# A decoder trunk in split float32: squares placed behind joins, pairs evacuated one behind the other, and norm sums taken by transposes

## The chip, the core and the metric

The kernel runs on one core of a Trainium2 chip. The metric is the device time of one execution in microseconds. Five engines work side by side, each through its own queue of instructions: PE (matrix products; its weight loads are listed as PEld), DVE (vector work), ACT (activations and copies), POOL and SP, which issues most DMAs. An instruction can wait for a semaphore that another engine raises; what stands behind it on its own engine waits with it.

## What is computed

Two layers of a decoder over 256 tokens of width 1024. Each layer is a half SwiGLU step, a token mixer, a cross attention over a memory of 256 rows, and a second half SwiGLU step, each behind an RMSNorm. The change concerns the norm and the first half step:

```python
def rmsnorm(x, g):
    x32 = x.astype(jnp.float32)
    y = x32 * lax.rsqrt(jnp.mean(x32 * x32, axis=-1, keepdims=True) + EPS)
    return y.astype(x.dtype) * g

def swiglu(x, w_gate, w_up, w_down):
    return (jax.nn.silu(x @ w_gate) * (x @ w_up)) @ w_down
...
    for l in range(DEPTH):
        x = x + 0.5 * swiglu(rmsnorm(x, ffn1_norm[l]), ffn1_w_gate[l], ffn1_w_up[l], ffn1_w_down[l])
```

The hidden width of SwiGLU is 2816, that is 22 column blocks of 128.

## The kernel before, in words

**Layout and products.** x lies transposed, as 8 row tiles of 128 features by 256 tokens. Every float32 factor is split into a high and a low part of a faster type: `hi` is a rounding copy on ACT, `lo` the difference on DVE. A product of a 128x128 weight tile with an x tile is then two matmuls (`mm`, L382 and L383): the high weight with both parts of x side by side, 512 columns, and the low weight with the high part of x, 256 columns. One column block takes 8 weight tiles, so 8 such pairs. `join` (L391) adds the two halves of the accumulator: ACT copies one half to SBUF (L392), DVE adds the other (L393).

**The weights.** `Stream` brings them in 1 MB chunks through SP into `raw` (4 buffers) and splits blocks of 8 tiles: `piece` issues the rounding copy `whi` on ACT (L127) and the difference `wlo` on DVE (L128). There are 5 buffers of each. `ws.fill()` splits the next block that is due, `ws.flush()` all that are due, `ws.take()` hands out a tile. Where in the code `fill` is called decides which other instructions the split is recorded among.

**The first half step** (`ffn` with `first=True`). `gates` computes the gate columns of blocks f0 to f3 in four accumulators while x and the weights still arrive. Then `gate_up` runs up f0, up f1, up f2, up f3, gate f4, up f4, gate f5, up f5, gate f6, up f6 and so on; each gets one of four `acc` buffers in PSUM and, once joined, one of eight `w1` buffers in SBUF. The products use x before it is normed; the norm's factor per token, `n.rbc`, is multiplied in afterwards. So a pair (gate, up) cannot be finished, nor its `w1` buffers freed, before `n.rbc` is there: `when_scaled` keeps its `evac` waiting. `evac(f)` is: gate times rbc (DVE, L516), silu (ACT, L517), `ws.fill()`, times up (DVE, L519), `ws.fill()`, and the split of the result into `h` (ACT L450, DVE L451).

**The norm's factor.** `squares` squares tiles of x on ACT (L327 two tiles at a time, L337 one) and adds them on DVE into one 128x256 tile, `sqacc`. `norm_scale` then makes the sum over the 128 partitions: `sums` multiplies each half of `sqacc` with a column of ones on PE (L346), DVE turns the two columns into mean plus epsilon (L348), POOL takes the power of minus one half (`rcol`, L350); `spread` transposes the broadcast `rcol` on PE (L356) and ACT copies it out as `rbc` (L358). The same function serves nine norms in the program, one of them that of the memory rows.

**What sets the order.** The program is recorded in the order of a hand-made planner (`Order`, method `after(delay, fn, cost)`, in planner nanoseconds): in the first half step, the squares are planned at 12000 to 17400, the sums at 18900. A scheduler then orders each engine's queue from a timing model of its own, keeping data dependencies; `tc.keep_in_program_order` takes an instruction out of that freedom. The cross attention (`attend_all`) has a step `go_weigh` that weights the values (L716 to L718).

## Time and profile before

| | us |
|---|---|
| median of 3 runs | 970.91 (970.76 to 971.05) |
| the profiled execution | 970.36 |
| its span, first to last instruction | 968.6 |
| PE busy in the span | 960.3 (99%) |
| DVE busy | 758.4 (78%) |
| ACT busy | 614.5 (63%) |
| POOL busy | 56.1 (6%) |

A row of the timeline gives start, duration, engine, line, operation, output and inputs, how many equal instructions were merged (x2), and in brackets how long the engine stood idle before it and what ended that. Durations overlap a little, since engines are pipelined: the distance between two starts is what a queue really takes. A row of the groups gives the count, then busy time and the mean in ns of one. PEclk is the granted clock of PE, 1.00 being full.

### The profile page before, as it was taken

The page shows a single profiled execution, that of the slowest core. Times are in us where ns is not written, and L with a number is a line of the kernel's source. Part 1 is how long each engine was busy: PE and PEld are TensorE (multiplying, and loading weights), DVE is VectorE, ACT ScalarE, POOL GpSimd, SP SyncE. Part 2 cuts the span into 40 slices and gives each one's busy share as a digit, 9 for nine tenths or more (in the row PEclk, how much of TensorE's full clock was granted, in tenths as well). Part 3 has the DMA queues.
Part 4 walks back from the last instruction along what each step waited for, and adds up shares of the span by engine and source line. Part 5 has one row for each costly group of instructions (what it writes and reads, how often), then busy time and mean ns, then how long its engine had stood idle before and what let it go on. Part 6 is the DMA issues. An engine that isn't in the chain of part 4 may idle for free.

```text
span 968.6 us, 16929 instructions
## 1 busy us (share of the span) xinstructions
PE 960.3 (99%) x6552; PEld 901.4 (93%) x6552; DVE 758.4 (78%) x1353; ACT 614.5 (63%) x1144; POOL 56.1 (6%) x95
## 2 busy tenths in 40 slices
PE   9999999999999999999999999999999999999997
PEld 8899999999999999999999999999999999999896
DVE  7988767798878888876778878677878789888663
ACT  7767655697658766665556666556786677666541
POOL 0410000002000000000000000000000004400011
PEclk9999999999999999999999999999999999999999
DMA  9797556555545665556555565565645357765631
GB/s 373 276 328 286 188 204 212 171 186 181 201 139 200 215 202 211 201 194 215 185 206 195 198 216 184 209 202 190 220 140 192 123 175 246 250 238 185 213 131 44
DMA packets 29921, 196.73 MB, mean 203 GB/s; under 512 B 3848, under 2 KB 4872, under 8 KB 7184
## 3 DMA queue, kind: packets, MB, share of 16 engines
q1 hardware_dynamic: 27072, 187.44, 55.6%
q0 software_dynamic: 2192, 7.37, 2.2%
q8 instruction: 51, 0.84, 0.4%
q10 hardware_dynamic: 576, 0.83, 0.2%
q14 instruction: 30, 0.25, 0.1%
HBM read 193.51 MB, written 5.27 MB: 205 GB/s over the span
## 4 chain that ended last, share of the span: by engine, by line
PE 99%; DVE 1%; ACT 0%; issue 0%; POOLq 0%; DVEq 0%; ACTq 0%
PE acc L382 42%; PE acc L383 21%; PE acc L387 7%; PE acc L389 7%; PE acc L388 7%; PE acc L565 1%; PE acc L564 1%; PE acc L563 1%; PE acc L905 1%; PE acc L907 1%; PE acc L906 1%; PE sc L563 0%; PE sc L565 0%; PE sc L564 0%; PE tr L289 0%; PE tr L740 0%
## 5 line engine op out<-in xcount | busy, mean ns | idle before, releaser
L127 ACT ACTIVATE whi<-raw 128x1024 fp32r<-128x1024 f32 (+2 forms) x377 | 369.5, 986 | 271.4 <-PE acc L382 132.0
L128 DVE TENSOR_TENSOR wlo<-raw,whi 128x1024 fp32r<-128x1024 f32 (+2 forms) x377 | 426.7, 1136 | 145.7 <-ACT whi L127 143.0
L382 PE MATMUL acc<-x,whi 128*128 128x512 f32 x1392 | 457.5, 383 | 0.5 <-DVE w L393 0.5
L383 PE MATMUL acc<-x,wlo 128*128 128x256 f32 x1392 | 377.6, 273 | 0.6 <-DVE wlo L128 0.6
L382 PEld LDWEIGHTS acc<-x,whi 128*128 128x128 f32 x1392 | 262.3, 189 | 36.8 <-PE acc L383 0.8
L383 PEld LDWEIGHTS acc<-x,wlo 128*128 128x128 f32 x1392 | 267.4, 192 | 1.8 <-DVE wlo L128 0.9
L382 PE MATMUL acc<-h,whi 128*128 128x512 f32 x462 | 151.3, 382 | 0.0
L383 PE MATMUL acc<-h,wlo 128*128 128x256 f32 x462 | 125.5, 273 | 0.0
L382 PEld LDWEIGHTS acc<-h,whi 128*128 128x128 f32 x462 | 87.1, 189 | 12.0
L383 PEld LDWEIGHTS acc<-h,wlo 128*128 128x128 f32 x462 | 88.7, 192 | 0.2
L388 PE MATMUL acc<-h,whi 128*128 128x256 f32 x322 | 87.8, 275 | 0.0
L389 PE MATMUL acc<-h,wlo 128*128 128x256 f32 x322 | 87.8, 275 | 0.0
L387 PE MATMUL acc<-h,whi 128*128 128x256 f32 x322 | 86.5, 277 | 0.0
L393 DVE TENSOR_TENSOR w<-acc,w 128x256 f32<-128x256 f32 x195 | 81.2, 417 | 3.8 <-ACT w L392 3.5
L389 PE MATMUL acc<-x,wlo 128*128 128x256 f32 x304 | 84.1, 278 | 0.0
L388 PE MATMUL acc<-x,whi 128*128 128x256 f32 x304 | 84.0, 278 | 0.0
L387 PE MATMUL acc<-x,whi 128*128 128x256 f32 x304 | 83.2, 278 | 0.0
L392 ACT ACTIVATE w<-acc 128x256 f32<-128x256 f32 x195 | 71.8, 369 | 9.2 <-PE acc L383 9.1
L388 PEld LDWEIGHTS acc<-h,whi 128*128 128x128 f32 x322 | 61.7, 192 | 0.1
L389 PEld LDWEIGHTS acc<-h,wlo 128*128 128x128 f32 x322 | 61.7, 192 | 0.1
L387 PEld LDWEIGHTS acc<-h,whi 128*128 128x128 f32 x322 | 60.6, 192 | 0.4 <-DVE x L445 0.2
L388 PEld LDWEIGHTS acc<-x,whi 128*128 128x128 f32 x304 | 58.2, 192 | 0.2
(207 smaller groups left out, 1181.5 us busy)
## 6 DMA issues: line engine op xcount, KB each, us to landing
raw<-in_w SPq DMA_DIRECT2D x171, 1024.0 KB, 5.0
dists<-line POOLq DMA_DIRECT2D x2, 1536.0 KB, 14.7
raw<-in_memT SPq DMA_DIRECT2D x3, 1024.0 KB, 4.9
raw<-in_w SPq DMA_DIRECT2D x6, 384.0 KB, 6.5
bias<-dists POOLq DMA_DIRECT2D x2, 1024.0 KB, 13.1
x<-in_xT SPq DMA_DIRECT2D x1, 1024.0 KB, 7.6
tok<-q POOLq DMA_DIRECT2D x32, 32.0 KB, 3.6
bias<-tok POOLq DMA_DIRECT2D x1, 1024.0 KB, 6.2
```

The lines of the kernel that those rows point to most:

```text
L127: for ins in (self.nc.scalar.activation(hi[:, at], src, AF.Copy), self.nc.vector.tensor_tensor(lo[:, at], src, hi[:, at].bitcast(F32), op= ...
L128: self.nc.vector.tensor_tensor(lo[:, at], src, hi[:, at].bitcast(F32), op=ALU.subtract)):
L382: nc.tensor.matmul(ps, w[0], x2.both, start=start, stop=False)
L383: nc.tensor.matmul(ps[:, :S], w[1], x2.high, start=False, stop=stop)
L387: nc.tensor.matmul(ps[:, :S], w[0], x2.high, start=start, stop=False)
L388: nc.tensor.matmul(ps[:, :S], w[0], x2.low, start=False, stop=False)
L389: nc.tensor.matmul(ps[:, :S], w[1], x2.high, start=False, stop=stop)
L392: nc.scalar.activation(halves(out), unpaired(ps[:, S:]), AF.Copy)
L393: nc.vector.tensor_tensor(halves(out), unpaired(ps[:, :S]), halves(out), op=ALU.add)
L563: nc.tensor.matmul(ps, hh, wh, start=f == 0, stop=False)
L564: nc.tensor.matmul(ps, hh, wl, start=False, stop=False)
L565: nc.tensor.matmul(ps, hl, wh, start=False, stop=f == FT - 1)
```

## The change

Four things are edited. `sums` transposes the halves of `sqacc` on PE, and DVE then adds along the rows (a reduce) before the same scaling; the column of ones is gone. In the first half step the squares are no longer planned by time but recorded right after the joins of up f0, f1 and f2, and `issue_after` orders each of them on its engine behind that join. `evac` of f0 to f4 is recorded inside `behind(*last_split)`: every DVE instruction of it, the `wlo` splits of its two `ws.fill()` included, is ordered behind the last split difference (DVE, L451) recorded before, which is that of the pair ahead. The sums are planned at 19500 instead of 18900. In the cross attention the first product of each weighting keeps its place in program order.

```diff
-                nc.tensor.matmul(pt[:, t:t + 1], n.acc[:, t * P:(t + 1) * P], ones, start=True, stop=True)
+                nc.tensor.transpose(pt[:, t * P:(t + 1) * P], n.acc[:, t * P:(t + 1) * P], ident)
             ms = act.tile([P, 2], F32, name="ms", bufs=2)
-            nc.vector.tensor_scalar(ms, pt[:, :2], 1.0 / D, EPS, op0=ALU.mult, op1=ALU.add)
+            nc.vector.tensor_reduce(ms, halves(pt[:, :S]), axis=AX.X, op=ALU.add)
+            nc.vector.tensor_scalar(ms, ms, 1.0 / D, EPS, op0=ALU.mult, op1=ALU.add)
...
+    @contextmanager
+    def behind(*instructions):
+
+        with ExitStack() as stack:
+            for ins in instructions:
+                stack.enter_context(tc.issue_after(ins.ins))
+            yield
...
     def split_into(x2, src):
 
         nc.scalar.activation(x2.hi, src, AF.Copy)
-        nc.vector.tensor_tensor(x2.lo, src, x2.hi.bitcast(F32), op=ALU.subtract)
+        last_split[:] = [nc.vector.tensor_tensor(x2.lo, src, x2.hi.bitcast(F32), op=ALU.subtract)]
         return x2
...
                     cur[f, part] = join(w1(), ps)
+                    if first and part == 1:
+                        with behind(*joined):
+                            for k in ((0, 1, 2, 3), (4, 5), (6, 7))[f] if f < 3 else ():
+                                squares(n, k, x)
...
-            nc.vector.tensor_tensor(g, g, n.rbc, op=ALU.mult)
-            nc.scalar.activation(g, g, AF.Silu)
-            ws.fill()
-            nc.vector.tensor_tensor(u, g, u, op=ALU.mult)
-            ws.fill()
-            h[f] = split_tile(halves(u))
-            ws.flush()
+            with behind(*(last_split if first and f <= SIDE else ())):
+                nc.vector.tensor_tensor(g, g, n.rbc, op=ALU.mult)
+                nc.scalar.activation(g, g, AF.Silu)
+                ws.fill()
+                nc.vector.tensor_tensor(u, g, u, op=ALU.mult)
+                ws.fill()
+                h[f] = split_tile(halves(u))
+                ws.flush()
...
-        if first:
-            for k in range(KT):
-                pe.after(12000 + 1800 * (k // 2), lambda k=k: squares(n, k, x), 0)
-        norm_scale(n, 18900 if first else 2300, unpin=True)
+        norm_scale(n, 19500 if first else 2300, unpin=True)
...
-                nc.tensor.matmul(out, vh, hi[:, u], start=u == 0, stop=False)
+                ins = nc.tensor.matmul(out, vh, hi[:, u], start=u == 0, stop=False)
+                if u == 0:
+                    tc.keep_in_program_order(ins)
```

How the queues change is seen at three places. (The line numbers of the changed kernel are higher: its joins are L399 and L400, its squares L325 and L335, the multiplications of `evac` L532 and L535, its split L461 and L462, its products L389 and L390; the spread is L355.)

The first is ACT in the first half step, from the join of the gate columns (`w1_236` to `w1_245`, from accumulators) to the weight splits of up f2 and up f3 (`whi_278`, `whi_282`). Before, the squares (`w2`, `sq`) stand ahead of the join of up f0 (`w1_271`):

```order
L392 ACTIVATE w1_245<-sc_169 128x256
L327 ACTIVATE w2_290<-x_69 128x512
L327 ACTIVATE w2_301<-x_69 128x512
L327 ACTIVATE w2_319<-x_69 128x512
L337 ACTIVATE sq_350<-x_69 128x256
L392 ACTIVATE w1_271<-acc_248 128x256
L127 ACTIVATE whi_278<-raw_163 128x1024
L127 ACTIVATE whi_282<-raw_163 128x1024
```

In the changed kernel the same stretch of ACT's queue, where `w1_269` is the join of up f0 and `whi_281`, `whi_285` are the splits of up f2 and up f3:

```order
L399 ACTIVATE w1_243<-sc_167 128x256
L399 ACTIVATE w1_269<-acc_246 128x256
L325 ACTIVATE w2_272<-x_69 128x512
L325 ACTIVATE w2_274<-x_69 128x512
L127 ACTIVATE whi_281<-raw_161 128x1024
L127 ACTIVATE whi_285<-raw_161 128x1024
L399 ACTIVATE w1_310<-acc_293 128x256
L325 ACTIVATE w2_313<-x_69 128x512
```

Two squares moved from ahead of the join to between the join and the weight splits, the others further back.

The second is DVE from the last weight splits ahead of the norm's factor onwards. Before, `wlo_406` belongs to gate f6 and `wlo_465` to up f6; L516 multiplies gates with `rbc`:

```order
L128 TENSOR_TENSOR wlo_406<-raw_325,whi_405 128x1024
L128 TENSOR_TENSOR wlo_465<-raw_325,whi_464 128x1024
L516 TENSOR_TENSOR w1_236<-w1_236,rbc_401 128x256
L516 TENSOR_TENSOR w1_239<-w1_239,rbc_401 128x256
L516 TENSOR_TENSOR w1_242<-w1_242,rbc_401 128x256
L516 TENSOR_TENSOR w1_245<-w1_245,rbc_401 128x256
L128 TENSOR_TENSOR wlo_546<-raw_388,whi_545 128x1024
```

In the changed kernel the weight split of gate f6 is `wlo_405`; the pair f0 (`w1_234` to `h_409`) and the joins of gate f4 and up f4 (`w1_438`, `w1_458`) come after it:

```order
L128 TENSOR_TENSOR wlo_405<-raw_323,whi_404 128x1024
L346 TENSOR_REDUCE ms_366<-tr_363 128x2
L347 TENSOR_SCALAR ms_366<-ms_366 128x2
L532 TENSOR_TENSOR w1_234<-w1_234,rbc_400 128x256
L535 TENSOR_TENSOR w1_269<-w1_234,w1_269 128x256
L462 TENSOR_TENSOR h_409<-w1_269,h_409 128x2x128
L532 TENSOR_TENSOR w1_237<-w1_237,rbc_400 128x256
L400 TENSOR_TENSOR w1_438<-acc_386,w1_438 128x256
L400 TENSOR_TENSOR w1_458<-acc_441,w1_458 128x256
```

and ten rows further on, on the same engine, the pair f3 (`w1_243` to `h_427`), the join of gate f6 (`w1_575`), and then the weight split of up f6, `wlo_464`:

```order
L532 TENSOR_TENSOR w1_243<-w1_243,rbc_400 128x256
L535 TENSOR_TENSOR w1_379<-w1_243,w1_379 128x256
L400 TENSOR_TENSOR w1_575<-acc_556,w1_575 128x256
L462 TENSOR_TENSOR h_427<-w1_379,h_427 128x2x128
L532 TENSOR_TENSOR w1_438<-w1_438,rbc_400 128x256
L128 TENSOR_TENSOR wlo_464<-raw_323,whi_463 128x1024
```

The weight split of up f6 stood ahead of the first multiplication with `rbc`; it now stands behind that multiplication and nineteen more instructions, the four waiting pairs among them.

The third is PE at the change from gate f6 to up f6. Before (`acc_557` gate f6, `acc_579` up f6):

```order
L382 MATMUL acc_557<-x_158,whi_405 128x512
L383 MATMUL acc_557<-x_158,wlo_406 128x256
L382 MATMUL acc_579<-x_111,whi_464 128x512
L383 MATMUL acc_579<-x_111,wlo_465 128x256
L382 MATMUL acc_579<-x_120,whi_464 128x512
```

In the changed kernel (`acc_556` gate f6, `acc_578` up f6, `acc_612` gate f7, `acc_634` up f7, `acc_668` gate f8):

```order
L389 MATMUL acc_556<-x_156,whi_404 128x512
L390 MATMUL acc_556<-x_156,wlo_405 128x256
L389 MATMUL acc_578<-x_109,whi_463 128x512
L389 MATMUL acc_612<-x_109,whi_544 128x512
L389 MATMUL acc_634<-x_109,whi_549 128x512
L389 MATMUL acc_668<-x_109,whi_600 128x512
L390 MATMUL acc_578<-x_109,wlo_464 128x256
```

Three first products of later column blocks moved ahead of the first product that reads `wlo_464`. The spread of the norm's factor (L355) stands directly ahead of gate f6 in the changed queue; before, its counterpart (L356) stood in the middle of up f4.

More of the change, by code (lines that the diff above doesn't have):

```diff
@@ L3 @@
 from collections import deque
-from contextlib import ExitStack
+from contextlib import ExitStack, contextmanager
 from itertools import chain
@@ L279, in build @@
     make_identity(nc, ident)
-    ones = consts.tile([P, 1], F32, name="ones")
-    nc.gpsimd.memset(ones, 1.0)
     mhalf = consts.tile([P, 2], F32, name="mhalf")
@@ L391, in join @@
     def join(out, ps):
-        nc.scalar.activation(halves(out), unpaired(ps[:, S:]), AF.Copy)
-        nc.vector.tensor_tensor(halves(out), unpaired(ps[:, :S]), halves(out), op=ALU.add)
+        joined[:] = (nc.scalar.activation(halves(out), unpaired(ps[:, S:]), AF.Copy),
+                     nc.vector.tensor_tensor(halves(out), unpaired(ps[:, :S]), halves(out), op=ALU.add))
         return out
+    joined = []
     def group(name, layer, c, n, evac, scaled=True):
@@ L446, in add_to_x @@
         normed_tile(nxt, j, x[:, j], x)
+    last_split = []
     def split_into(x2, src):
         nc.scalar.activation(x2.hi, src, AF.Copy)
-        nc.vector.tensor_tensor(x2.lo, src, x2.hi.bitcast(F32), op=ALU.subtract)
+        last_split[:] = [nc.vector.tensor_tensor(x2.lo, src, x2.hi.bitcast(F32), op=ALU.subtract)]
         return x2
```

## The prediction

> **What bounds the kernel now.** I read the page first: its line of busy times, then the share of the chain that ended last.
>
> ```profile
> PE 960.3 (99%) x6552; PEld 901.4 (93%) x6552; DVE 758.4 (78%) x1353; ACT 614.5 (63%) x1144; POOL 56.1 (6%) x95
> PE 99%; DVE 1%; ACT 0%; issue 0%; POOLq 0%; DVEq 0%; ACTq 0%
> ```
>
> PE is busy 960.3 us of 968.6 and carries 99% of the chain. So only two things can move the time: PE work that goes or comes, and waits of PE. Next I read PE's timeline for rows with an idle time in brackets.
>
> ```profile
> 22.70 0.38 PE L383 MATMUL acc<-x,wlo 128*128 128x256 f32 x1 [0.60 <-DVE wlo L128]
> ...
> 38.43 0.38 PE L382 MATMUL acc<-x,whi 128*128 128x512 f32 x1
> 38.65 0.27 PE L383 MATMUL acc<-x,wlo 128*128 128x256 f32 x1
> 39.42 0.45 PE L382 MATMUL acc<-x,whi 128*128 128x512 f32 x1 [0.50 <-DVE w L393]
> ```
>
> PE waits twice in the middle. At 22.70 it waits for the weight split of up f2, at 39.42 (gate f6) for a join that frees an accumulator. The products of one column block start 2.62 us after those of the block before:
>
> ```profile
> 33.19 0.38 PE L382 MATMUL acc<-x,whi 128*128 128x512 f32 x1
> ```
>
> From this row to 38.43 lie sixteen pairs of products in 5.24 us, so 0.327 us a pair and 2.62 us a block of eight. A second product follows its first by 0.22 (38.43 to 38.65), and a new pair follows 0.11 later. Gate f6 could have begun at 38.76; it began at 39.42, a wait of 0.66. Both waits lie where the change moves instructions.
>
> **Part 1: the sums (a gain of 2.0).** Three rows of PE around one sum, three around a spread, which is two transposes of the shape that the changed sums use, then the rows of the tiles and the nearest reduce.
>
> ```profile
> 323.23 0.50 PE L346 MATMUL tr<-ones,sqacc 128*128 128x1 f32 x4
> 323.59 0.46 PE L382 MATMUL acc<-x,whi 128*128 128x512 f32 x1
> 323.89 0.27 PE L383 MATMUL acc<-x,wlo 128*128 128x256 f32 x1
> ...
> 103.80 0.38 PE L356 MATMUL tr<-ident,rcolm 128*128 128x128 f32 x2
> 103.94 0.46 PE L382 MATMUL acc<-x,whi 128*128 128x512 f32 x1
> 104.24 0.27 PE L383 MATMUL acc<-x,wlo 128*128 128x256 f32 x1
> ...
> L348 DVE TENSOR_SCALAR ms<-tr x9: 148/152/159, 28.1 to 799.4; 128x2 f32<-128x2 f32 x9
> L350 POOL TENSOR_TENSOR rcol<-ms,mhalf x8: 689/1004/1614, 28.4 to 799.7; 128x2 f32<-128x2 f32 x8
> ...
> L672 DVE TENSOR_REDUCE neg<-sc 128x2 f32<-128x512 f32 x8 | 5.5, 692 | 3.5 <-PE sc L666 3.5
> ```
>
> From the sum to the second product behind it takes 0.66 us (323.23 to 323.89); from the two transposes to the same product 0.44 (103.80 to 104.24). The difference is 0.22 a sum, and nine sums (`ms` x9) give 9 x 0.22 = 2.0 us of PE, all on the path. The added reduce of 256 columns costs DVE at most the 0.69 of the reduce of 512; with POOL's 0.7 to 1.6 it makes some 2.3 us at most from sum to spread, and in the changed queue PE has over 4 us of products between them. I take it as hidden. Uncovered, the 0.69 would come back nine times, 6 us, but nothing near that distance is left out.
>
> **Part 2: the squares and the first wait (a loss of 0.3).**
>
> ```profile
> 17.18 1.70 ACT L327 ACTIVATE w<-x 128x512 f32<-128x512 f32 x3
> 18.74 0.44 ACT L337 ACTIVATE sq<-x 128x256 f32<-128x256 f32 x1
> 19.29 0.38 ACT L392 ACTIVATE w<-acc 128x256 f32<-128x256 f32 x1
> 19.57 1.99 ACT L127 ACTIVATE whi<-raw 128x1024 fp32r<-128x1024 f32 x2
> ...
> 21.43 2.35 DVE L128 TENSOR_TENSOR wlo<-raw,whi 128x1024 fp32r<-128x1024 f32 x2
> ```
>
> Before, three double squares and a single fill the 2.1 us ahead of the join of up f0 (17.18 to 19.29), which waits for PE in any case. In the changed queue ACT idles there, and two double squares stand between that join and the weight splits of up f2 and up f3. Double squares start 0.52 apart (18.74 less 17.18, by three), so the splits start at 19.57 + 2 x 0.52 = 20.61. Before, DVE's `wlo` of up f2 began at 21.43, though its `whi` was done at 20.63 (19.57 and 1.06): DVE had other work. So 0.8 of the delay of 1.04 is absorbed: now `whi` ends at 21.67, and `wlo`, which takes 1.22, runs from 21.7 to 22.94 where it ended at 22.65 before. PE continues at 23.0 instead of 22.70: 0.3 more, from 0 (the joins come sooner too) to 1.0 (all of the two squares).
>
> **Part 3: the second wait (a loss of 8.4).** This carries the forecast. The rows are the sum, its use, and the means of the instructions in a pair's chain.
>
> ```profile
> 27.18 0.50 PE L346 MATMUL tr<-ones,sqacc 128*128 128x1 f32 x4
> ...
> 32.41 0.38 ACT L358 ACTIVATE rbc<-tr 128x256 f32<-128x256 f32 x1 [0.36 <-PE tr L356]
> 33.22 1.42 DVE L516 TENSOR_TENSOR w<-w,rbc 128x256 f32<-128x256 f32 x4
> 40.53 0.41 DVE L516 TENSOR_TENSOR w<-w,rbc 128x256 f32<-128x256 f32 x1
> 40.97 0.42 ACT L517 ACTIVATE w<-w 128x256 f32<-128x256 f32 x1 [0.37 <-DVE w L516]
> ...
> L128 DVE TENSOR_TENSOR wlo<-raw,whi 128x1024 fp32r<-128x1024 f32 x316 | 386.2, 1224 | 140.1 <-ACT whi L127 138.3
> L127 ACT ACTIVATE whi<-raw 128x1024 fp32r<-128x1024 f32 x316 | 332.9, 1057 | 258.1 <-PE acc L382 127.8 <-ACT h L450 61.2 <-PE acc L565 24.2
> L393 DVE TENSOR_TENSOR w<-acc,w 128x256 f32<-128x256 f32 x195 | 81.2, 417 | 3.8 <-ACT w L392 3.5
> L392 ACT ACTIVATE w<-acc 128x256 f32<-128x256 f32 x195 | 71.8, 369 | 9.2 <-PE acc L383 9.1
> L519 DVE TENSOR_TENSOR w<-w,w 128x256 f32<-128x256 f32 x88 | 36.6, 423 | 7.8 <-DVE w L393 0.9
> L451 DVE TENSOR_TENSOR h<-w,h 128x256 fp32r<-128x256 f32 x96 | 39.3, 415 | 0.0
> L450 ACT ACTIVATE h<-w 128x256 fp32r<-128x256 f32 x96 | 38.2, 406 | 2.9 <-DVE w L519 1.4 <-DVE w L871 1.4
> ```
>
> Before, the factor is there at 32.8, and DVE works the four pairs side by side (four multiplications in 1.42, 0.36 apart) while PE is at up f4 and gate f5. In the changed queue the spread stands directly ahead of gate f6, at 38.76 + 0.3 (part 2) - 0.22 (the sum) - 0.22 (its own transposes) = 38.6. ACT has a weight split ahead of `rbc` (`whi` of gate f8), whose buffer is read by up f5's last first product, at 38.3 now (38.43 + 0.3 - 0.44); that ends at 38.7, the split a microsecond later, `rbc` at 40.05. DVE's first multiplication starts at 40.1.
>
> Now the pairs go one behind the other. One pair is a multiplication, silu, a multiplication, a copy, a difference: five steps of 0.41 to 0.42, and each needs the one before from the other engine; the rows at 40.53 and 40.97 show 0.03 between such steps. That is 2.2 us a pair. Joins go between.
>
> - Pair f0: 40.1 to 42.3. Gate f4's join needs the `w1` buffer that pair f0 frees, and DVE does it behind f1's first multiplication: 42.57 to 42.98. Only then is gate f4's accumulator free, which gate f6 takes. PE starts gate f6 at 43.1 instead of 38.76 + 0.3 - 0.22 = 38.84: a wait of 4.25.
> - Pair f1 to 44.55, pair f2 to 47.1, with the joins of up f4, gate f5 and up f5 and a multiplication of f5 among them on DVE. Pair f3 starts at 47.03; its second multiplication ends at 48.34.
> - ACT has `whi` of up f8 and its half of gate f6's join there: 47.8 to 48.75 to 49.12. DVE: the join to 49.57, f3's difference to 49.9, f4's multiplication to 50.2, and then at last the weight split of up f6, 50.16 to 51.37.
> - PE reaches up f6 at 43.1 + 2.62, takes four advanced first products (0.22 each, 0.87) and stands at 46.6 until 51.43.
>
> Without waits PE would be there at 38.84 + 2.62 + 0.87 = 42.33. The two waits together are 51.43 - 42.33 = 9.1, in place of 0.66: 8.4 more. What is queued behind the waits on DVE, the weight splits up to gate f8, follows without a gap at 1.22 each against 2.62 that a block takes on PE, so I see no further wait; the eleven us from `rbc` to the split are worth some 1 us either way, by handoffs of 0 to 0.08 at twenty steps.
>
> **Part 4: the clock (a loss of 0.4).** The only place in the trace where PE runs dry for long is the end.
>
> ```profile
> 962.21 0.28 PE L565 MATMUL acc<-whi,h 128*128 128x256 f32 x1
> ...
> 960.00:965.00 5.00, 2.48 (x23) 2.29 (x21) 3.43 (x11) 1.08 (x2) 1.43 (x2) 0.99 0.30 105
> 965.00:970.00 5.00, 0.00 (x0) 0.00 (x0) 0.12 (x1) 0.06 (x1) 0.00 (x0) 0.50 0.30 105
> ```
>
> In these rows of windows the granted clock is third from the right: 0.99 for 960 to 965, 0.50 from 965. 0.99 of 5 us at levels of 1.00 and 0.50 means 0.1 us at half, so the clock fell at about 964.9, some 2.4 us after the last product ended at 962.49. The first wait of 4.25 us is longer. If gate f6 then runs at half clock, its 2.62 us become up to 5.24, an estimate that takes a product to slow with the clock; no row has a product at half clock. Most of this lies under the wait for the weight split: only `whi` of up f8, which needs gate f6's last first product, slips from 47.8 to 48.2, and with it all behind: 0.4. From 0 (the clock holds) to a whole block at half clock behind the wait (a rival below).
>
> The Trainium skill, page "TensorE: Matmul & The Clock Gate", section "Part 1: The HAM clock gate (the "warmup" mystery)", says that the clock falls to half after an idle window of about 3.4 us, and that about 3.4 us of sustained work brings it back. The trace's fall after 2.4 us is earlier than a whole window. By the page a wait of 4.25 us would bring the fall too, and half clock could outlast gate f6.
>
> **Part 5: the weightings (0).**
>
> ```profile
> L701 ACT ACTIVATE p<-tr 128x512 fp32r<-128x512 f32 x8 | 4.8, 599 | 2.9 <-PE tr L699 2.9
> ```
>
> Eight weightings (`p` x8) keep their place. One pair of products less (0.22) lies between their last transposes and them, some 1.3 us, which the copy (0.60) and a difference of about as much just fill. I take 0; uncovered, up to 0.22 each, 1.8.
>
> **The sum.** 0.3 + 8.4 + 0.4 - 2.0 = +7.1. The profiled execution took 970.36, so 977.5; the median, 970.91, is 0.55 above it, so 978.0.
>
> **The rivals.**
>
> - **Half clock stays.** The fall outlasts the waits and the rest of up f6 runs at half clock: the block less its first second-product, 2.4 us more. For it: the fall at 964.9; against it: no row shows how long it stays. 980.4. The page named above gives this result, if its sustained time counts from up f6 on.
> - **Only the accumulator is waited for.** If DVE reached up f6's split in time, only the 4.25 would stand: 0.3 + 4.25 - 0.66 - 2.0 = +1.9, 972.8. Against it: nineteen rows behind the first multiplication in DVE's queue.
> - **Faster: the pairs end before they are needed.** If `rbc` came so early that the chain of 11.3 us (40.05 to 51.37) ended by 42.3, both waits would go: 0.3 - 0.66 - 2.0 = -2.4, 968.5. It decides at `rbc` by 31.0, earlier than the 32.41 of before. Against it: the spread stands ahead of gate f6. Should `behind` not hold the split back, this too is the outcome; the order shows that it does.
> - **The weightings wait.** 1.8 more: 979.8. For it: the small slack; against it: PE shows no such idle now.
>
> **How the numbers follow.** The forecast has 0.62, half clock 0.18, the weightings 0.10, the accumulator alone 0.05, faster 0.05. Least and most are the forecast's 977 and 979, for handoffs and the first wait, then the two dearer rivals up to 980.4, and their sum, handoffs included, up to 982; downwards, half of a pair's time in part 3 gives 976. About 0.2% (1.9 us) is what a measurement can tell from no change: 968.5 lies outside, 972.8 just inside, all else is slower by more.
>
> **What would show it.** PE's timeline should have an idle of about 4 us ahead of gate f6, released by a join, and one of 2 to 5 us inside up f6, released by a `wlo`; the first wait about 0.9; sums followed 0.44 later by their second product; PEclk below 1.00 near 45. I am wrong if DVE's timeline has `wlo` of up f6 ahead of the pairs, if `rbc` comes before 35, or if PE's idle time beyond the start and the end is under 5 us.

## The result, and the profile after

The changed kernel takes 982.14 us (median of 4 runs, 980.53 to 982.51) against 970.84 for the kernel before in the same comparison. The ratio is 1.0114, with a 95% interval of 1.0102 to 1.0127: it is slower by 11.3 us, where 7.1 were forecast. The profiled execution took 981.79 us, 11.4 more than that of before. Three of the four executions, the profiled one among them, took 981.79 to 982.51 us at a mean granted clock of 0.993; the fourth took 980.53 at 0.996.

The line of the changed kernel's page that gives the busy time by engine:

```profile
PE 964.0 (98%) x6534; PEld 902.7 (92%) x6534; DVE 760.1 (78%) x1362; ACT 614.7 (63%) x1144; POOL 52.1 (5%) x94
```

The span is 980.0 us. So PE is idle 16.0 us where it was idle 8.3, which is 7.7 of the loss. PE is also *busy* 3.7 us longer, although the sums were to make it 2.0 us shorter. That is the first sign that some of its work ran slower.

PE's timeline of the changed kernel in the first half step. In brackets stands the idle time ahead of a row and what ended it:

```profile
21.10 0.27 PE L390 MATMUL acc<-x,wlo 128*128 128x256 f32 x1
...
22.37 0.48 PE L389 MATMUL acc<-x,whi 128*128 128x512 f32 x1 [0.46 <-ACT whi L127]
22.74 0.38 PE L390 MATMUL acc<-x,wlo 128*128 128x256 f32 x1
...
38.35 0.38 PE L355 MATMUL tr<-ident,rcol 128*128 128x128 f32 x2
42.85 0.77 PE L389 MATMUL acc<-x,whi 128*128 128x512 f32 x1 [4.12 <-DVE w L400]
...
43.63 0.63 PE L389 MATMUL acc<-x,whi 128*128 128x512 f32 x1
44.27 0.63 PE L389 MATMUL acc<-x,whi 128*128 128x512 f32 x1
...
49.98 0.48 PE L389 MATMUL acc<-x,whi 128*128 128x512 f32 x1 [0.59 <-DVE w L400]
51.78 0.38 PE L390 MATMUL acc<-x,wlo 128*128 128x256 f32 x1 [1.32 <-DVE wlo L128]
...
54.09 0.63 PE L389 MATMUL acc<-x,whi 128*128 128x512 f32 x1
54.73 0.63 PE L389 MATMUL acc<-x,whi 128*128 128x512 f32 x1
```

Gate f6 starts at 42.85, released by a join, and the first product with up f6's weight split at 51.78, released by that split. The forecast had 43.1 and 51.43. In gate f6, behind the first of the two waits, pairs of products start 0.64 apart (43.63 to 44.27) instead of 0.327. At 54.09 and 54.73, behind both waits, they do so again.

The granted clock is the third number from the right in the rows of windows:

```profile
42.00:44.00 2.00, 1.15 (x3) 1.05 (x4) 1.52 (x6) 1.34 (x4) 1.49 (x9) 0.56 0.05 9
44.00:46.00 2.00, 2.00 (x8) 1.67 (x7) 1.95 (x6) 1.20 (x5) 2.00 (x10) 0.50 0.00 0
...
48.00:50.00 2.00, 1.41 (x6) 0.81 (x4) 0.89 (x3) 1.63 (x3) 0.29 (x2) 0.74 0.09 12
50.00:52.00 2.00, 0.68 (x3) 0.39 (x4) 2.00 (x4) 0.42 (x1) 1.85 (x5) 1.00 0.52 141
52.00:54.00 2.00, 2.00 (x9) 1.70 (x9) 2.00 (x3) 0.00 (x0) 0.30 (x1) 0.62 0.99 326
54.00:56.00 2.00, 2.00 (x9) 1.73 (x8) 2.00 (x3) 0.42 (x1) 0.00 (x0) 0.53 1.06 197
```

A mean between 0.50 and 1.00 tells when the level changed: 0.56 over 2 us is 1.76 us at half, so the clock fell at 42.24. By the same reckoning it came back at 49.04 (0.74), fell again at 52.48 (0.62) and came back at 55.88 (0.53). It was at half for 6.8 us and then for 3.4. The second stretch is full of products; since pairs start twice as far apart at half, 3.4 us do the work of 1.7, so it costs 1.7 us.

The chain of the factor and the pairs, on ACT and DVE of the changed kernel:

```profile
39.41 0.36 ACT L357 ACTIVATE rbc<-tr 128x256 f32<-128x256 f32 x1
...
39.80 0.42 DVE L532 TENSOR_TENSOR w<-w,rbc 128x256 f32<-128x256 f32 x1 [4.67 <-ACT rbc L357]
42.29 0.75 DVE L400 TENSOR_TENSOR w<-acc,w 128x256 f32<-128x256 f32 x2
...
50.51 3.48 DVE L128 TENSOR_TENSOR wlo<-raw,whi 128x1024 fp32r<-128x1024 f32 x3
```

DVE waits 4.67 us for `rbc`. It joins gate f4 at 42.29, which frees the accumulator for gate f6, and reaches up f6's weight split at 50.51, 10.7 us behind the first multiplication.

Last, the residual additions of the first layer: the last one of the mixer and the first four of the cross attention. First before, then after, with the product that waits there:

```profile
274.11 0.41 DVE L445 TENSOR_TENSOR x<-acc,x 128x256 f32<-128x256 f32 x1
307.79 1.41 DVE L445 TENSOR_TENSOR x<-acc,x 128x256 f32<-128x256 f32 x4 [0.39 <-PE acc L389]
```

```profile
284.23 0.41 DVE L454 TENSOR_TENSOR x<-acc,x 128x256 f32<-128x256 f32 x1
319.04 1.41 DVE L454 TENSOR_TENSOR x<-acc,x 128x256 f32<-128x256 f32 x4
...
315.43 0.71 PE L394 MATMUL acc<-h,whi 128*128 128x256 f32 x4 [0.81 <-ACT h L461]
```

The changed kernel is 10.12 us behind at the end of the mixer and 11.25 behind at the residual additions of the cross attention: 1.13 lost in between. A product of the output projection waits there for the split (`h`) of a weighting. The same wait of 0.81 stands in the second layer, at 791.04.

### The profile page after: what moved, and what is told of

Its sections match the earlier page's. It is cut to its first block, busy times and chain, and to the rows that moved or that the text cites. A ratio compares the mean times of both kernels' runs of the same rounds, so it can differ in the third digit from the quotient of the medians.

```text
span 980.0 us, 16898 instructions
## 1 busy us (share of the span) xinstructions
PE 964.0 (98%) x6534; PEld 902.7 (92%) x6534; DVE 760.1 (78%) x1362; ACT 614.7 (63%) x1144; POOL 52.1 (5%) x94
## 4 chain that ended last, share of the span: by engine, by line
PE 97%; DVE 1%; ACT 1%; DMA 0%; issue 0%; POOLq 0%; SPq 0%; DVEq 0%; ACTq 0%
PE acc L389 41%; PE acc L390 21%; PE acc L395 7%; PE acc L396 7%; PE acc L394 7%; PE acc L581 1%; PE acc L580 1%; PE acc L579 1%; PE acc L921 1%; PE acc L922 1%; PE acc L920 1%; PE sc L579 0%; PE sc L581 0%; PE sc L580 0%; DMA raw<-in_w 0%; ACT whi L127 0%
## 5 line engine op out<-in xcount | busy, mean ns | idle before, releaser
L389 PE MATMUL acc<-x,whi 128*128 128x512 f32 x1392 | 462.0, 386 | 5.6 <-DVE w L400 4.7
L390 PE MATMUL acc<-x,wlo 128*128 128x256 f32 x1392 | 378.9, 274 | 1.3 <-DVE wlo L128 1.3
L389 PEld LDWEIGHTS acc<-x,whi 128*128 128x128 f32 x1392 | 264.2, 191 | 43.5 <-issue 4.3
L390 PEld LDWEIGHTS acc<-x,wlo 128*128 128x128 f32 x1392 | 269.0, 193 | 2.8 <-DVE wlo L128 1.8
L389 PE MATMUL acc<-h,whi 128*128 128x512 f32 x462 | 151.3, 382 | 0.0
L390 PE MATMUL acc<-h,wlo 128*128 128x256 f32 x462 | 125.4, 273 | 0.0
L389 PEld LDWEIGHTS acc<-h,whi 128*128 128x128 f32 x462 | 87.1, 189 | 12.0
L390 PEld LDWEIGHTS acc<-h,wlo 128*128 128x128 f32 x462 | 88.7, 192 | 0.2
L400 DVE TENSOR_TENSOR w<-acc,w 128x256 f32<-128x256 f32 x195 | 81.0, 417 | 5.8 <-ACT w L399 5.4
L399 ACT ACTIVATE w<-acc 128x256 f32<-128x256 f32 x195 | 71.9, 369 | 12.1 <-PE acc L390 11.6
```

What stands on the lines that cost most here:

```text
L389: nc.tensor.matmul(ps, w[0], x2.both, start=start, stop=False)
L390: nc.tensor.matmul(ps[:, :S], w[1], x2.high, start=False, stop=stop)
L399: joined[:] = (nc.scalar.activation(halves(out), unpaired(ps[:, S:]), AF.Copy), nc.vector.tensor_tensor(halves(out), unpaired(ps[:, :S]), ...
L400: nc.vector.tensor_tensor(halves(out), unpaired(ps[:, :S]), halves(out), op=ALU.add))
```

## The experiments

Each kernel was timed beside the kernel before on the same chip. The kernel before took 970.67 us beside the first three kernels below and the one without the weightings' kept place; 970.83 beside those with the late squares alone, the clock kept up, the sums alone and the seven sums; and 970.84 beside the other four.

### Pairs free, squares late

```diff
-            with behind(*(last_split if first and f <= SIDE else ())):
+            with behind():
```

> The changed kernel, with evac no longer recorded inside behind; all else stays. In DVE's queue the weight splits up to gate f8 now stand ahead of the first multiplication with rbc and the four pairs go side by side, but the spread of the norm's factor still stands directly ahead of gate f6. Theory A (the order of the pairs makes the wait): both waits go, about 971.4 us (970.9 before, 0.3 for the first wait, -2.0 for the sums, +2.2 for the cross attention). Theory B (the factor is late, because squares and sums are): rbc is there at about 39.4, the split of gate f8 and four multiplications go first, so gate f4's accumulator comes free at about 44 and gate f6 waits about 5.5 us, somewhat longer than the 4.2 of the changed kernel; only the wait inside up f6 goes. About 978.5 us.

Measured: 978.77 us, ratio 1.0082 (1.0067 to 1.0097). Theory B holds. ACT, DVE and PE of this kernel:

```profile
40.00 0.36 ACT L357 ACTIVATE rbc<-tr 128x256 f32<-128x256 f32 x1
41.27 1.43 DVE L532 TENSOR_TENSOR w<-w,rbc 128x256 f32<-128x256 f32 x4
44.29 0.42 DVE L400 TENSOR_TENSOR w<-acc,w 128x256 f32<-128x256 f32 x1
44.85 0.77 PE L389 MATMUL acc<-x,whi 128*128 128x512 f32 x1 [5.52 <-DVE w L400]
```

The pairs go side by side (four multiplications in one row), so the first is done later, and gate f6 waits 5.52 us instead of 4.12. The wait inside up f6 is gone. The order of the pairs is not what makes the wait at gate f6; a factor that comes at 40.0 is.

### Pairs in order, weight splits free

```diff
-            with behind(*(last_split if first and f <= SIDE else ())):
-                nc.vector.tensor_tensor(g, g, n.rbc, op=ALU.mult)
-                nc.scalar.activation(g, g, AF.Silu)
-                ws.fill()
-                nc.vector.tensor_tensor(u, g, u, op=ALU.mult)
-                ws.fill()
-                h[f] = split_tile(halves(u))
-                ws.flush()
+            order = last_split if first and f <= SIDE else ()
+            with behind(*order):
+                nc.vector.tensor_tensor(g, g, n.rbc, op=ALU.mult)
+                nc.scalar.activation(g, g, AF.Silu)
+            ws.fill()
+            with behind(*order):
+                nc.vector.tensor_tensor(u, g, u, op=ALU.mult)
+            ws.fill()
+            with behind(*order):
+                h[f] = split_tile(halves(u))
+            ws.flush()
```

> The changed kernel, with the multiplications and the split of each evac still behind the pair ahead, but its two ws.fill() outside, so that the weight splits are free of that order: up f6's now stands ahead of the first multiplication with rbc. Theory of the prediction (two waits in a row, one for an accumulator, one for up f6's weight split): the second goes, the first stays or grows by the 0.8 us of the one split that now stands ahead of pair f0; the clock still falls in gate f6, but not a second time. About 978 us (976.5 to 979.5). Rival (the chain of pairs sets the end, the fills only lie in it): as the changed kernel, 982.

Measured: 977.92 us, ratio 1.0076 (1.0061 to 1.0091). The first theory holds to 0.1 us. PE of this kernel has one wait left, for the join that follows pair f0:

```profile
44.38 0.77 PE L389 MATMUL acc<-x,whi 128*128 128x512 f32 x1 [4.99 <-DVE w L400]
```

The clock falls only once here: its means are 0.78, 0.50, 0.50 and 0.51 in the windows of 2 us from 42 to 50, and 1.00 from 50 on. So the second wait, with the clock that it brings down, is worth 982.1 - 977.9 = 4.2 us of the change, although the first wait has grown, and it comes from the weight splits recorded inside the order (the two `ws.fill()` and the `ws.flush()`) alone.

### Squares early, pairs in order with the fills

```diff
-                    if first and part == 1:
-                        with behind(*joined):
-                            for k in ((0, 1, 2, 3), (4, 5), (6, 7))[f] if f < 3 else ():
-                                squares(n, k, x)
...
-        norm_scale(n, 19500 if first else 2300, unpin=True)
+        if first:
+            for k in range(KT):
+                pe.after(12000 + 1800 * (k // 2), lambda k=k: squares(n, k, x), 0)
+        norm_scale(n, 18900 if first else 2300, unpin=True)
```

> The changed kernel, with squares and sums planned by time as before (12000 to 17400, 18900); the pairs still go one behind the other with the fills inside. Theory A (the order of the pairs with the fills in it makes the wait by itself): rbc at about 32.8, the chain of pairs with its joins, which wait for gate f6 as well, ends at about 44.5 with up f6's weight split, where PE would be at 42.3: a wait of 2 to 2.5 us inside up f6 and none ahead of gate f6, about 973 us. Theory B (only the late factor does it): no wait, about 970.6 us (970.9 - 2.0 for the sums + 2.2 for the cross attention - 0.6 for the wait at gate f6).

Measured: 979.80 us, ratio 1.0093 (1.0076 to 1.011). Neither number. The rows of ACT and PE:

```profile
35.49 0.39 ACT L357 ACTIVATE rbc<-tr 128x256 f32<-128x256 f32 x1
45.43 0.48 PE L389 MATMUL acc<-x,whi 128*128 128x512 f32 x1 [2.16 <-DVE w L400]
48.60 0.58 PE L390 MATMUL acc<-x,wlo 128*128 128x256 f32 x1 [2.69 <-DVE wlo L128]
```

There is no wait at the start of gate f6, as theory A said, and PE waits inside up f6 (45.43 is an advanced product of gate f8, 48.60 up f6 itself). But `rbc` came at 35.49, not at 32.8, the two waits are 4.85 us, and the clock fell during them (its mean is 0.81 in the window from 46 to 48, 0.50 from 48 to 54). Why `rbc` is late although the squares are early is shown by the sums alone, below. The kind of theory A holds: with the fills in it, the order of the pairs makes PE wait without any late squares. That it would do so with the factor at its old time, too, is not shown: no run has the fills in the order with the sums of before.

### Squares late, nothing else

The squares and the planned time of the sums as in the change, the rest as before:

```diff
+                    if first and part == 1:
+                        with behind(*joined):
+                            for k in ((0, 1, 2, 3), (4, 5), (6, 7))[f] if f < 3 else ():
+                                squares(n, k, x)
...
-        if first:
-            for k in range(KT):
-                pe.after(12000 + 1800 * (k // 2), lambda k=k: squares(n, k, x), 0)
-        norm_scale(n, 18900 if first else 2300, unpin=True)
+        norm_scale(n, 19500 if first else 2300, unpin=True)
```

> The kernel before with only the squares behind the joins and the sums planned at 19500; pairs, sums and weightings as before. Theory (the late factor alone makes PE wait for gate f4's accumulator): as the changed kernel without behind in evac, less the sums' gain and the loss in the cross attention, which about cancel: 978.5 us, a wait of about 5.5 us ahead of gate f6, half clock behind it. Rival (the squares as such only lengthen the first wait): 971.1 us.

Measured: 978.42 us, ratio 1.0079 (1.0065 to 1.0092). PE:

```profile
45.08 0.77 PE L390 MATMUL acc<-x,whi 128*128 128x512 f32 x1 [5.52 <-DVE w L401]
```

The move of the squares, with the later plan of the sums that goes with it, costs 7.6 us by itself; the two were not taken apart. It and the order of the pairs with the fills (in the kernel above) are each enough for long waits around gate f6 and up f6. Their costs, 7.6 and 9.1 us, don't add up to that of the change: the likely reason, not tested by itself, is that the pairs run while PE is waiting for the late factor anyway.

### The clock kept up

```diff
     pe = Order()
+    pe.busy = False
...
             nc.scalar.activation(n.rbc, pt[:, :S], AF.Copy)
+            if unpin and not pe.busy:
+                pe.busy = True
+                busy(n.rbc[:, :P], 12)
...
+    def busy(src, count):
+        pt = tr_tile()
+        for _ in range(count):
+            nc.tensor.matmul(pt[:, :P], warm, src, start=True, stop=True)
...
                 h[f] = split_tile(halves(u))
+                if first and f in {2: 8, 3: 8}:
+                    busy(u[:, :P], {2: 8, 3: 8}[f])
```

> The changed kernel with idle products on PE while it waits: 12 behind the norm's factor and ahead of gate f6, 8 and 8 inside up f6, each 128x128 on data that is there by then; nothing reads them. Theory (half clock costs, beside the waits): gate f6 still starts at about 42.9 and up f6's weight split still comes at about 51.4, but the clock does not fall; the 1.7 us of the second fall and some 0.4 of the first come back: 980.0 us. Rival (the fall lies wholly in time that PE waits anyway): 982, the same as the changed kernel.

Measured: 980.93 us, ratio 1.0103 (1.009 to 1.0117), 1.2 us under the changed kernel. PE's timeline and windows (each idle product is listed as two, so twelve are x24):

```profile
23.02 0.48 PE L398 MATMUL acc<-x,whi 128*128 128x512 f32 x1 [0.46 <-ACT whi L127]
40.47 2.94 PE L378 MATMUL tr<-rbc,warm 128*128 128x128 f32 x24 [1.09 <-ACT rbc L358]
52.28 0.38 PE L399 MATMUL acc<-x,wlo 128*128 128x256 f32 x1 [0.33 <-DVE wlo L128]
```

```profile
44.00:46.00 2.00, 2.00 (x14) 1.84 (x13) 1.52 (x6) 1.44 (x4) 2.00 (x13) 1.00 0.00 0
54.00:56.00 2.00, 2.00 (x14) 1.84 (x13) 2.00 (x3) 1.12 (x2) 0.00 (x0) 1.00 0.92 221
```

The clock stays at 1.00 in both stretches, and in all windows from 36 to 58. This profile is 0.65 us later than the changed kernel's at the first wait already (23.02 against 22.37). From there up f6's split comes 29.26 us later, against 29.41 (51.78 less 22.37): the slow gate f6 cost 0.15, not the 0.4 forecast, and the rest of what comes back is the second fall. The eight pairs of up f6 from that product on take 4.29 us in the changed kernel (51.78 to 56.07) and 2.62 here (52.28 to 54.90), so the second fall costs 1.67 there. In the two profiled executions that is 980.93 against 981.79, 0.86, and 0.65 for the start, together 1.5 where 2.1 were expected. Half clock costs, and most of the cost lies behind the waits.

### The weightings' place, out and alone

In the first of these two kernels the kept place is taken out of the change, in the second it is put alone into the kernel before:

```diff
-                if u == 0:
-                    tc.keep_in_program_order(ins)
```

> The changed kernel without keeping the first product of each weighting in program order. In the changed kernel a product of the output projection waits 0.8 us for the split of a weighting, once a layer, and PE falls back 1.1 us there. Theory A (keeping the place causes that): it goes, about 979.9 us. Theory B (the sums by transposes changed the order around it, and the kept place only moves the wait): both weightings of the pair stand side by side, and the second waits for its weights' split instead, about as long; 982 us, within 0.5.

> The kernel before with only the first product of each weighting kept in program order. In its queue one weighting of the last pair then stands six products later, and the output projection's products that need its neighbour stand ahead of it. Theory (the kept place by itself costs, as 2 x 0.67 us of the changed kernel's loss suggested): 971 to 972.2 us, a wait of a product for the split of a weighting, once a layer. Rival (it costs only together with the sums, since without them the products ahead cover it): 970.8, no change.

Measured: 980.17 us (ratio 1.0098, 1.0083 to 1.0113) without it, nearly theory A; 972.06 us (1.0014, 1.0005 to 1.0023) with it alone, as its theory said. The first median lies between two kinds of executions, though: two took 980.8 us at a mean granted clock of 0.994, two 979.5 at 0.997. Beside the changed kernel's at 0.993 and 0.996, like with like, taking the kept place out gains 1.5 and 1.0 us on average and not the 2.0 between the medians. PE of the kernel without it still waits, elsewhere, for a weighting's `p`:

```profile
315.71 0.38 PE L729 MATMUL tr<-p,bias 128*128 128x256 f32 x1 [0.74 <-DVE p L715]
```

In the kernel with it alone, a product of the output projection waits for a weighting's split, in both layers, and DVE's residual additions come later:

```profile
306.25 0.38 PE L388 MATMUL acc<-h,whi 128*128 128x256 f32 x1 [0.16 <-DVE h L451]
...
274.62 0.42 DVE L445 TENSOR_TENSOR x<-acc,x 128x256 f32<-128x256 f32 x1
308.99 1.41 DVE L445 TENSOR_TENSOR x<-acc,x 128x256 f32<-128x256 f32 x4
```

This kernel is 0.51 behind before at 274.62 and 1.20 behind at 308.99: the kept place costs 0.69 a layer. Only 0.16 of it is listed as idle time; the starts of the products next to that row (305.15 to 306.47) lie 0.65 us further apart in all than the usual 0.11. The rest of the 1.13, about 0.45, comes from the sums: the kernel with the sums alone, below, takes 34.11 us from the one addition to the other (274.95 to 309.06) against 33.68 before.

### The sums alone, in seven norms, and folded

All nine sums by transposes and VectorE in the kernel before, as in the change:

```diff
-                nc.tensor.matmul(pt[:, t:t + 1], n.acc[:, t * P:(t + 1) * P], ones, start=True, stop=True)
+                nc.tensor.transpose(pt[:, t * P:(t + 1) * P], n.acc[:, t * P:(t + 1) * P], ident)
...
-            nc.vector.tensor_scalar(ms, pt[:, :2], 1.0 / D, EPS, op0=ALU.mult, op1=ALU.add)
+            nc.vector.tensor_reduce(ms, halves(pt[:, :S]), axis=AX.X, op=ALU.add)
+            nc.vector.tensor_scalar(ms, ms, 1.0 / D, EPS, op0=ALU.mult, op1=ALU.add)
```

> The kernel before with the sums by transposes and VectorE alone. Theory of the prediction: nine sums give 9 x 0.22 = 2.0 us of PE and the reduce is hidden; the cross attention, whose order the sums change, takes back the 0.45 us a layer that the changed kernel without the kept place showed: 970.8 - 2.0 + 0.9 = 969.7 us. Rival (the reduce, on the way from sums to spread, is not hidden): 0.4 to 0.6 us back nine times, 973 us or more.

Measured: 971.26 us, ratio 1.0004 (0.9995 to 1.0013). No gain. DVE, ACT and PE of this kernel:

```profile
28.42 0.41 DVE L348 TENSOR_REDUCE ms<-tr 128x2 f32<-128x256 f32 x1
28.75 1.21 DVE L128 TENSOR_TENSOR wlo<-raw,whi 128x1024 fp32r<-128x1024 f32 x1
29.89 0.41 DVE L394 TENSOR_TENSOR w<-acc,w 128x256 f32<-128x256 f32 x1
30.22 0.15 DVE L349 TENSOR_SCALAR ms<-ms 128x2 f32<-128x2 f32 x1
...
34.68 0.38 ACT L359 ACTIVATE rbc<-tr 128x256 f32<-128x256 f32 x1
...
40.71 0.45 PE L383 MATMUL acc<-x,whi 128*128 128x512 f32 x1 [1.70 <-DVE w L394]
```

The reduce itself takes 0.41. But a weight split and a join stand between it and the scaling of its result, `rbc` comes at 34.68 instead of 32.41, and gate f6 waits 1.70 instead of 0.50. (0.3 of the 2.3 us lie before: this profile's first wait ends at 23.02, against 22.70.) In the cross attention PE waits 0.74 us for a weighting's `p`, as in the kernel without the kept place. 1.2 and 2 x 0.45 take back the 2.0; the measured loss of 0.4 is a little more than that.

In the next kernel the norms ahead of the cross attention keep the product with ones; their `norm_scale` is the only one called with `wide=False`:

```diff
-                nc.tensor.matmul(pt[:, t:t + 1], n.acc[:, t * P:(t + 1) * P], ones, start=True, stop=True)
+                if wide:
+                    nc.tensor.transpose(pt[:, t * P:(t + 1) * P], n.acc[:, t * P:(t + 1) * P], ident)
+                else:
+                    nc.tensor.matmul(pt[:, t:t + 1], n.acc[:, t * P:(t + 1) * P], ones, start=True, stop=True)
```

> The kernel before with the sums by transposes for seven of the nine norms; the two norms ahead of the cross attention keep the product with ones. The order of the products in the cross attention is then that of before. Theory (the loss in the cross attention comes from the order of its products, which the sums of its own norm change): no loss there, 7 x 0.22 = 1.5 us gained: 969.3 us, a little faster than with all nine. Rival (the loss comes with sums by transposes anywhere): 970.8 - 1.5 + 0.9 = 970.2.

Measured: 970.24 us, ratio 0.9991 (0.9982 to 1.0). That is the rival's number, but not by its cause: nothing is lost in the cross attention. From the mixer's last addition to those of the cross attention it takes 33.67 us, as before (33.68). The gain is eaten by the wait at gate f6 (1.70 again, 1.2 more than before) and by one of 0.58 for the power of the memory's norm, on PE:

```profile
192.89 0.43 PE L363 MATMUL tr<-ident,rcol 128*128 128x128 f32 x2 [0.58 <-POOL rcol L357]
```

These two waits are worth more than the 1.5 us of the seven sums. In the profiles the span from the end of the first wait on is indeed 0.35 us longer than before (946.25 against 945.90); the kernel reaches that point 0.45 earlier (22.25 against 22.70), for a reason that no run shows. So as far as the profiles show, the 0.6 us that this kernel gains are not what the sums bring on PE.

In the last kernel of this kind the scaling goes:

```diff
-            nc.scalar.activation(sq, stream[:, k - 1:k + 1].rearrange("p k s -> p (k s)"), AF.Square)
+            nc.scalar.activation(sq, stream[:, k - 1:k + 1].rearrange("p k s -> p (k s)"), AF.Square, scale=1.0 / 32)
...
+                nc.vector.scalar_tensor_tensor(n.acc, sq, EPS / P, n.acc, op0=ALU.add, op1=ALU.add)
...
+                nc.vector.tensor_reduce(ms, halves(pt[:, :S]), axis=AX.X, op=ALU.add)
```

> As the seven sums by transposes, with the scaling folded away: the squares are taken of x/32, the smallest addend enters with the last square, and DVE's second instruction on the sums is gone, so that no weight split can stand between the reduce and POOL's power. In the run with seven sums alone such a split and a join stood there, rbc came 2.3 us later behind the sums than before and gate f6 waited 1.7 us instead of 0.5. Theory (that second instruction is what takes the gain): rbc comes as before, gate f6 waits 0.5 again, no wait for rcol in the memory's norm: 970.8 - 1.5 = 969.3 us. Rival (the reduce itself is late, or the gain of PE is not there): 970.2, as with seven sums.

Measured: 969.31 us, ratio 0.9985 (0.9976 to 0.9994), as the theory said. ACT and PE:

```profile
33.27 0.38 ACT L367 ACTIVATE rbc<-tr 128x256 f32<-128x256 f32 x1 [0.91 <-PE tr L365]
39.75 0.45 PE L391 MATMUL acc<-x,whi 128*128 128x512 f32 x1 [0.50 <-DVE w L402]
```

Gate f6 waits 0.50 as before, PE no longer waits for the power in the memory's norm, and the seven sums bring their 1.5 us. This kernel beats both.

### Pairs in order with early squares, alone and with the folded sums

The order of the pairs with the fills outside, as in the second experiment, in the kernel before and in the last one. Of each `evac`, without the fills:

```diff
-            nc.vector.tensor_tensor(g, g, n.rbc, op=ALU.mult)
-            nc.scalar.activation(g, g, AF.Silu)
+            order = last_split if first and f <= SIDE else ()
+            with behind(*order):
+                nc.vector.tensor_tensor(g, g, n.rbc, op=ALU.mult)
+                nc.scalar.activation(g, g, AF.Silu)
```

> The kernel before with the pairs f0 to f4 one behind the other in DVE's queue (multiplications and split of each evac), but with the weight splits of ws.fill() outside that order; squares, sums and weightings as before. The splits of gate f6 and up f6 stand ahead of the first pair, the following ones between its steps. Theory (a pair at a time frees the first accumulator sooner, and harms only where weight splits are queued behind pairs or the factor is late): gate f6's wait of 0.66 goes, nothing else changes: 970.2 us. Rival (one pair at a time is slower as such, and some accumulator or split comes late): 972 or more.

> The two runs with the folded sums and with the pairs one behind the other, together. If both theories hold: 970.8 - 1.5 - 0.6 = 968.7 us, faster than both kernels. If one of the two falls: 969.3 or 970.2; if the pairs harm, more.

Measured: 971.08 us (ratio 1.0002, 0.9993 to 1.0011) and 969.43 us (0.9986, 0.9977 to 0.9995). The times alone barely tell 971.08 from the 970.2 of the theory, but the wait does: the theory that a pair at a time frees the first accumulator sooner falls. Rows of ACT, DVE and PE of the first of the two:

```profile
36.04 1.06 ACT L127 ACTIVATE whi<-raw 128x1024 fp32r<-128x1024 f32 x1 [1.32 <-PE acc L391]
37.00 0.40 ACT L459 ACTIVATE h<-w 128x256 fp32r<-128x256 f32 x1
38.27 0.42 DVE L460 TENSOR_TENSOR h<-w,h 128x256 fp32r<-128x256 f32 x1
...
38.94 0.42 DVE L402 TENSOR_TENSOR w<-acc,w 128x256 f32<-128x256 f32 x1
39.51 0.45 PE L391 MATMUL acc<-x,whi 128*128 128x512 f32 x1 [0.83 <-DVE w L402]
```

Pair f0's copy stands behind a weight split on ACT that itself waits for PE to free a buffer. The pair is paced by PE's reading of weights and not by its own five steps. Its split comes at 38.27, 15.8 us behind the end of the first wait (22.46), just as in the kernel before (38.52 behind 22.70). The join that frees the accumulator (38.94) now has a multiplication of the next pair ahead of it (38.61), and gate f6 waits 0.83 instead of 0.50.

## Why the prediction was right, and where it was not

**What bounds the kernel.** Right: of the 11.4 us between the two profiles, 7.7 are idle time of PE and 3.7 are longer busy time of PE.

**The sums.** The size on PE is right: seven of them, with nothing else disturbed, bring the 1.5 us that 7 x 0.22 gives. "I take it as hidden", of the reduce, is right for the changed kernel: POOL's power is done at 36.00 there, and the spread, which needs it, stands at 38.35 in PE's queue without a wait of its own. It fails in the kernel before, and not by the reduce's duration: the second instruction on its result is queued behind a weight split and a join.

**The first wait.** Right in size: 0.3 was forecast and 0.33 came. From the last product of up f1 to the first second product of up f2 it takes 1.64 us in the changed kernel (21.10 to 22.74). In the kernel before it takes 1.31, from this row to the one at 22.70:

```profile
21.39 0.27 PE L383 MATMUL acc<-x,wlo 128*128 128x256 f32 x1
```

With the late squares alone it is 1.64, too (21.70 to 23.34). Where it shows was wrong: not as an idle time of 0.9 ahead of a product that needs the `wlo`, but as one of 0.46 ahead of an advanced product that needs a `whi`, and as wider starts beside it. The absolute times can't tell it: profiles that share this stretch of the change pass the wait between 22.37 and 23.03.

**The second wait.** Right in mechanism, in places and in when PE goes on: 42.85 and 51.78 where 43.1 and 51.43 stood, a join and a weight split as releasers. Taking the fills out of the order removes the second wait, as the step says. The sign "one of 2 to 5 us inside up f6" did not come: 1.32 us, and 0.59 ahead of it for another join. PE's idle time in the two waits is 6.0 us and not 9.1, because at half clock gate f6 and the advanced products up to 49.39 took 6.5 us of what was forecast as 3.5 us of work and a longer wait; the split that sets the end came hardly later for it. What the step left open is which part of the change to blame. The late squares alone cost 7.6 us, the order of the pairs with the fills 9.1 with early squares, though the sums' late factor and the weightings are in that. The rival for "faster" asked for a factor by 31.0; no run has one so early with the fills in the order, and at 35.49 the pairs with their fills still came late.

**The clock.** This is one of the two steps that were mis-sized. The fall under gate f6 was forecast at 0.4 and cost 0.15, since it lay under the wait. But "a whole block at half clock behind the wait" was left to a rival at 2.4 us and a chance of 0.18, and it came, in another form. The fall did not outlast the waits, as that rival has it: the clock came back at 49.04, while PE ran the advanced products between its waits, and fell again at 52.48, when the waits were over, for 3.4 us that cost 1.7. No line of the prediction has a second fall. The rule from the Trainium skill, page "TensorE: Matmul & The Clock Gate", section "Part 1: The HAM clock gate (the "warmup" mystery)", speaks of windows of about 3.4 us that run on their own: the stretches of 6.8, 3.4 and 3.4 us between the changes agree with it.

**The weightings.** The other mis-sized step: taken at 0, "uncovered, up to 0.22 each". They cost 2 x 1.13 = 2.3. The price was looked for at the weighting's own wait for its `p`. It lies one step on, at the product of the output projection that needs the split of the weighting (`h`), in a stretch of PE's queue that the step didn't look at. Of it 0.69 a layer is the kept place, the rest the sums.

**The sum.** Forecast were 7.1, with a chance of 0.62 for 977 to 979 us, and that did not come. With the first fall at 0.15, the second fall's 1.7 and the weightings' 2.3 it is 10.8; 11.3 were measured, so about 0.5 us are left without a place. The time lies at the very end of the range, 982, which was the sum of the two dearer rivals (2.4 and 1.8). That it holds is partly luck: what came were 1.7 and 2.3, each by another way than its rival describes. The execution of 980.53 us with the higher mean clock is near what the forecast and the weightings give without the second fall (970.84 + 7.1 + 2.3 = 980.2), so the second fall may not come in every execution; only one was profiled, and this is not shown.

## What to carry to other kernels

A constraint that orders a helper's instructions also orders everything recorded inside it: here the calls that refill weight buffers turned a preference among four pairs into a wait of the busiest engine. When an engine that carries the chain runs dry for several microseconds, count the slower clock behind the wait too. And when one instruction on a short chain becomes two, look at what a scheduler will put between them before calling the first one hidden.

## What the runs showed of the hardware that was not expected

The clock can fall because of waits that are already over. In the stretch from 49.04 to 52.48 PE was idle for 0.59 and 1.32 us, 1.9 of 3.4, and the fall came at its end, when PE was busy again. A single wait of 1.70 us ahead of 40.71 in the kernel with the sums alone left the clock at 1.00 in every window from 36 to 50. If the clock is judged in stretches of 3.4 us that follow one another, the kernel with late squares alone says a little more: it fell at 44.40 (a mean of 0.60 from 44 to 46), and the last stretch but one ahead of that, 37.6 to 41.0, held the first 1.4 us of the wait and brought no fall. So the idle time that brings one would lie between 1.4 and 1.9 us of 3.4; the runs don't settle it more closely.

The clock comes back late, too: a stretch that is nearly full was not enough. Reckoned as above, the first stretch at half lasted 6.8 us in every profile with a fall under these waits: 42.24 to 49.04 in the changed kernel, 42.44 to 49.28 with the pairs free, 43.12 to 49.96 with the splits free, 47.24 to 54.08 with early squares, 44.40 to 51.24 with late squares alone. In the first half of it PE was idle for only 0.6 us in the changed kernel (42.24 to 42.85), and the clock did not come back; it came back at the end of the second half, in which PE had no idle time, and likewise after 3.4 us of products behind the second fall.

At half clock a pair of products took 0.64 us against 0.327, so it slows in proportion, which no row of the kernel before showed.
